# Filling the start of a two-layer decoder trunk: idle transposes, an earlier gate weight, small loads last

## The chip, the cores and the metric

The kernel runs on one core of a Trainium2 chip. What counts is the device time in microseconds (us) of one execution: the median of several.

## The reference

A trunk of two layers on x (1 x 1024 x 1024, float32). Layer 1 mixes tokens with a gated linear recurrence (HGRN2, 8 heads of 128), layer 2 with sliding-window attention; each has a gated feed-forward part behind it, and every sub-layer ends with a layer norm. Only the head of layer 1 matters here:

```python
def hgrn2_mixer(h, w_in, lower_bound, g_norm_w, w_out):
    """h (B,S,D); w_in (D, 4D) = [q | f | i | g] columns"""
    q, f, i, g = jnp.split(h @ w_in, 4, axis=-1)
    ...
    fg = lb + (1.0 - lb) * jax.nn.sigmoid(heads(f))
    o = hgrn2_chunkwise(jax.nn.silu(heads(q)), 1.0 - fg, heads(i), jnp.log(fg))
    o = o * lax.rsqrt(jnp.mean(jnp.square(o), -1, keepdims=True) + RMS_EPS)
    o = o * g_norm_w.astype(jnp.float32) * jax.nn.silu(heads(g))
    return o.reshape(B, S, D).astype(h.dtype) @ w_out
```

So every head needs x times four blocks of 128 columns of `w_in`: i, g, q and f.

## The kernel before, in words

**Tiling.** x is held as eight blocks of 128 rows ("rows 0" to "rows 7"). Every product needs x with the model dimension on the partitions, so each block is transposed on TensorE (`x_block`, through `tr`, L179: eight transposes of 128 x 128 into one PSUM tile `psax`) and then split into a high and a low part in `T` (`split`: ScalarE makes the high part, L196, VectorE the low part, L144). A product of float32 quality is three matmuls, high x high, high x low, low x high (`mm3`, L169 to L171).

**Weights.** A weight block of 512 KB is loaded into one of three `raw` buffers in turn (`load`, L139) and split into one of six slots of `HL` (`split_raw`: ScalarE L151, then VectorE L144; for the first one GpSimd). `ig_load(h, u)` takes half of the model dimension of i and g of head h with two DMAs of 256 KB; `qf_load(h, g)` takes the whole of q (g = 0) or f (g = 1) with one DMA.

**Stages at the beginning.** Rows 0 and 1 are transposed; then the i/g projection of head 0 runs in four blocks of two row blocks each (`ig_block(0, us, tp)`, tp = 0 to 3: "block 0" to "block 3"), with the transposes of the next two row blocks set among its matmuls (`x_pair`, a chain of the `Order` object that steps when the counted TensorE time has passed). A block has 48 matmuls of 256 columns and, for blocks 0 to 2, 16 transposes. Then come the f and q projection of head 0 and, head by head, the recurrence. Between blocks 2 and 3 the parameters (`pr`, 81 x 128) are transposed into `par` (L745), and before that the masks (`mf`) are turned into bytes (`msk`, L743).

**Who sets the order.** Inside `tc.manual_schedule(engines=...)` the named engines keep the order in which the program is written. For engines that aren't named a scheduler chooses the place of each instruction by its own estimate of when it can start; this is so for ScalarE and VectorE where head 0's f and q weights are split, since that code names only TensorE and SyncE. All loads of this stage go through SyncE's queue (SP), in the order written, and eight semaphores take turns: a DMA is only issued when the DMA eight places ahead of it has landed.

The lines around the change in the kernel before:

```python
                ahead = od.spawn(x_pair(2), 2.0)
                ig_block(0, us, 0)
                od.finish([ahead])
                for i, n in enumerate(("hgrn_lb_logits", ...)):
                    nc.sync.dma_start(pr[16 * i:16 * (i + 1), :], ...)
                nc.sync.dma_start(pr[80:81, :], a["hgrn_gnorm_w"])
                for tb in range(4, NB):
                    x_load(tb)
...
            w = {g: qf_split(qf_load(0, k)) for k, g in enumerate("qf")}
```

Of the kernel before, what the change touches and what calls it, by code (L numbers as in the profile page):

```python
# [10 lines left out]
F32 = mybir.dt.float32  # L11
# [5 lines left out]
P = 128  # L17
S = 1024
D = 1024
NB = S // P  # L20
KC = D // P
BL = 32
# [65 lines left out]
def trunk(ctx: ExitStack, tc: tile.TileContext, a: dict, out: bass.AP):  # L88
    nc = tc.nc
# [13 lines left out]
    ident = cp.tile([P, P], F32, name="ident")  # L103
# [11 lines left out]
    def psmm():  # L115
        return mmp.tile([P, 512], F32, name="psmm")

    def psax():
        return axp.tile([P, 1024], F32, name="psax")
# [12 lines left out]
    def hl_at(i):  # L132
        return HL[:, 2 * i:2 * i + 2, :]

    def load(loads):
        raw = tail["raw"][ring["raw"] % 3]
        ring["raw"] += 1
        for view, src in loads(raw):
            nc.sync.dma_start(view, src)  # L139
        return raw  # L140
# [9 lines left out]
    def split_into(hl, raw, eng=None):  # L150
        nc.scalar.copy(hl[:, 0], raw)  # L151
        low_part(hl[:, 1], raw, hl[:, 0], eng)
        return hl

    def split_raw(raw, eng=None):
        ring["hl"] += 1
        return split_into(hl_at((ring["hl"] - 1) % 6), raw, eng)
# [20 lines left out]
    def tr(ps, src):  # L178
        nc.tensor.transpose(ps, src, ident)  # L179
        od.t += 0.109  # L180
# [14 lines left out]
    def split(hi, lo, src, eng=None):  # L195
        nc.scalar.copy(hi, src)  # L196
        return low_part(lo, src, hi, eng)
# [462 lines left out]
    w_in = a["hgrn_w_in"][0]  # L660
    w_iv = w_in.rearrange("(kc p) c -> p kc c", p=P)
    hgrn_pool = tc.tile_pool(name="hp", bufs=1, reuse_waits="tile")
    with tc.tile_pool(name="t", bufs=1, reuse_waits="tile") as raws, hgrn_pool as hp:
        raw_tail(raws)

        def ig_load(h, u):
            return load(lambda r: [(r.rearrange("p (k g c) -> p k g c", k=4, g=2)[:, :, g, :],
                                    w_iv[:, 4 * u:4 * u + 4, (2 + g) * D + h * P:(2 + g) * D + (h + 1) * P])
                                   for g in range(2)])

        def ig_split(raw, eng=None):
            return split_raw(raw, eng).rearrange("p h (k c) -> p h k c", k=4)

        VG = {}

        def ig_block(h, us, tp):
            if tp == 0:
                VG[h] = (hp.tile([P, NB, P], F32, name="V"), hp.tile([P, NB, P], F32, name="G"))
            V, G = VG[h]
            ps = psmm()  # L680
# [16 lines left out]
        with tc.tile_pool(name="ep", bufs=1, reuse_waits="tile") as ep:  # L697
            pr = ep.tile([81, P], F32, name="pr")

            def x_load(tb):  # L700
                nc.sync.dma_start(Y[:, tb, :], x[tb * P:(tb + 1) * P, :])

            def x_block(tb):
                ps = psax()
                for kc in range(KC):
                    tr(ps[:, kc * P:(kc + 1) * P], Y[:, tb, kc * P:(kc + 1) * P])
                ts = slice(tb * P, (tb + 1) * P)
                split(T[:, 0, :, ts], T[:, 1, :, ts], ps.rearrange("p (k t) -> p k t", k=KC))

            def x_pair(tb):  # L710
                yield 0.0
                x_block(tb)
                yield 0.5
                x_block(tb + 1)

            warm = sm.tile([P, 1], F32, name="warm")
            nc.scalar.copy(warm, nhalf)
            with tc.manual_schedule(engines={EN.PE, EN.SP, EN.Activation, EN.DVE}):
                x_load(0)
                raw0 = ig_load(0, 0)  # L720
                x_load(1)
                raw1 = ig_load(0, 1)
                for tb in range(2, 4):
                    x_load(tb)
                us = [ig_split(raw0, nc.gpsimd)]
                x_block(0)
                x_block(1)
                us.append(ig_split(raw1))
                ahead = od.spawn(x_pair(2), 2.0)
                ig_block(0, us, 0)  # L730
                od.finish([ahead])
                for i, n in enumerate(("hgrn_lb_logits", "ln_mix_g", "ln_mix_b", "ln_ffn_g", "ln_ffn_b")):
                    nc.sync.dma_start(pr[16 * i:16 * (i + 1), :], a[n].rearrange("r (k p) -> (r k) p", p=P))
                nc.sync.dma_start(pr[80:81, :], a["hgrn_gnorm_w"])
                for tb in range(4, NB):
                    x_load(tb)
            for tp in range(1, NB // 2 - 1):
                ahead = od.spawn(x_pair(2 * tp + 2), 2.0)
                ig_block(0, us, tp)
                od.finish([ahead])  # L740
            mf = hp.tile([P, 7 * BL + P], F32, name="kd")
            nc.sync.dma_start(mf, a["masks"])
            nc.vector.tensor_copy(msk, mf)  # L743
            ps = psmm()
            nc.tensor.transpose(ps[:, :81], pr, ident[:81, :81])  # L745
            nc.vector.tensor_copy(par, ps[:, :81])
            lm = ep.tile([P, NH], F32, name="lm")
            le = ep.tile([P, 2, NH], F32, name="le")
            nc.vector.tensor_tensor(lm, par[:, 0:8], par[:, 8:16], op=ALU.max)
            for r in range(2):  # L750
                nc.vector.tensor_tensor(le[:, r, :], par[:, 8 * r:8 * r + 8], lm, op=ALU.subtract)
            nc.scalar.activation(le, le, AF.Exp)
            nc.vector.tensor_tensor(lm, le[:, 0, :], le[:, 1, :], op=ALU.add)
            nc.vector.reciprocal(lm, lm)
            nc.vector.tensor_tensor(lbt[:, 0, :], le[:, 0, :], lm, op=ALU.mult)
            nc.vector.tensor_scalar(lbt[:, 1, :], lbt[:, 0, :], -1.0, 1.0, op0=ALU.mult, op1=ALU.add)
            ig_block(0, us, NB // 2 - 1)
# [25 lines left out]
            nc.scalar.dma_start(rbd, rl.unsqueeze(1).to_broadcast([16, P, 2 * P]))  # L783

        params = od.spawn(conv_params())

        def qf_load(h, g):
            wv = w_in.rearrange("(kc p) c -> p kc c", p=P)
            c0 = g * D + h * P
            return load(lambda r: [(r.rearrange("p (k c) -> p k c", k=KC), wv[:, :, c0:c0 + P])])  # L790

        def qf_split(raw):
            return split_raw(raw).rearrange("p h (k c) -> p h k c", k=KC)

        def qf(h, weights):

# [18 lines left out]
        def recur(h, qs, fg, kp):  # L815
# [98 lines left out]
            yield 2.2  # L914
            V, G = VG[h]
            ps = psax()
# [86 lines left out]

        values_done = [-1]
        with tc.manual_schedule(engines={EN.PE, EN.SP}):
            w = {g: qf_split(qf_load(0, k)) for k, g in enumerate("qf")}
            nw, nraw = {}, {g: qf_load(1, k) for k, g in ((1, "f"), (0, "q"))}
            make_w = [lambda g=g: nw.update({g: qf_split(nraw[g])}) for g in "fq"]
            steps = qf(0, w)
            for k in range(4):  # L1010
                slot_begin()
                slot_end(*next(steps), *(make_w[k - 1:k] if k else ()))
            for _ in steps:
                pass
            task = od.spawn(recur(0, *w["out"]))
            w = nw
            for h in range(1, NH):
                us, nw = [], {}
                raws = [ig_load(h, u) for u in range(2)]
                make_ig = [lambda u=u: us.append(ig_split(raws[u])) for u in range(2)]  # L1020
                steps = qf(h, w)
                for make in ((), make_ig[:1], make_ig[1:], ()):
                    slot_begin()
                    slot_end(*next(steps), *make)
                for _ in steps:
                    pass
                if h < NH - 1:
                    nraw = {g: qf_load(h + 1, k) for k, g in ((1, "f"), (0, "q"))}
                    make_w = [lambda g=g: nw.update({g: qf_split(nraw[g])}) for g in "fq"]
                else:  # L1030
                    make_w = []
                for tp in range(NB // 2):
                    if tp == lead[h]:
                        od.finish([task])
                        task = od.spawn(recur(h, *w["out"]))
                    slot_begin()
                    slot_end(*ig_block(h, us, tp), *(make_w[tp - 1:tp] if tp else ()))
                w = nw
# [41 lines left out]
    with (tc.tile_pool(name="ta", bufs=1, reuse_waits="tile") as raws,  # L1080
# [195 lines left out]
        with tc.manual_schedule(engines={EN.PE, EN.Activation, EN.DVE, EN.Pool}):  # L1276
# [12 lines left out]
            g = q_proj(hl)  # L1289
            q, done = next(g)  # L1290
# [11 lines left out]
            for c in range(8):  # L1302
# [31 lines left out]
                q = nq  # L1334
# [58 lines left out]
```

## Time and profile before

| | us |
|---|---|
| median of 3 runs | 2213.2 |
| lowest and highest | 2210.26, 2213.62 |
| the profiled execution | 2211.82 |
| its span | 2209.8 |

The span is the time from the first to the last instruction in the trace; the profiled execution's own time is 2.0 us longer. Times in the views count from the span's start. In a timeline a row is start, duration, engine, line, operation, what is written from what, and in brackets how long the engine was idle before it and what ended that. In a table of windows a row is the stretch, its length, busy time and number of instructions of TensorE's matmuls (PE), weight loads (PEld), VectorE (DVE), ScalarE (ACT) and GpSimd (POOL), then the granted TensorE clock, the DMA engines' share and GB/s. The trace has no record of the clock ahead of 12.17 us, so the column says nothing there.

### The profile page before, as it was taken

The numbers are of one execution on the slowest core, as the hardware profiler recorded it, in microseconds if no ns is written. First come the engines' busy times: TensorE is split into PE (matmuls) and PEld (weight loads), VectorE is DVE, ScalarE is ACT, GpSimd is POOL, SyncE is SP. The second block draws the span as 40 slices with busy tenths as digits, with TensorE's granted clock in tenths as the row PEclk, the third lists the DMA queues.
The fourth block names the chain that finished last, engine by engine and source line by source line (L and its number), as shares of the span: only waits on it lengthen the run. The fifth ranks groups of instructions, "written<-read, shape, count | busy, mean of one in ns | idle before, by whom it ended". The sixth has DMA issues, their size and how long they took to land.

```text
span 2209.8 us, 33157 instructions
## 1 busy us (share of the span) xinstructions
PE 2168.1 (98%) x13007; PEld 1810.5 (82%) x13007; DVE 1777.6 (80%) x2415; ACT 932.1 (42%) x1601; POOL 178.6 (8%) x196
## 2 busy tenths in 40 slices
PE   8999999989999999999999999999999999999998
PEld 7888888878888888887888888878888888887887
DVE  2777665555789888988997779977899888889987
ACT  4333333332744334344343546655654444343431
POOL 0122111110100000000000013211000000000001
PEclk9999999999999999999999999999999999999999
DMA  6565443152223222227954431123123222249663
GB/s 197 173 208 195 161 168 120 48 97 89 96 69 104 86 86 86 86 79 252 303 162 153 106 99 35 34 81 120 67 96 105 80 73 77 86 153 315 202 208 137
DMA packets 231942, 281.14 MB, mean 127 GB/s; under 512 B 29977, under 2 KB 160746, under 8 KB 228970
## 3 DMA queue, kind: packets, MB, share of 16 engines
q1 hardware_dynamic: 228898, 276.57, 38.6%
q10 hardware_dynamic: 2888, 2.45, 0.9%
q8 instruction: 102, 1.67, 0.3%
q14 instruction: 54, 0.44, 0.1%
HBM read 213.96 MB, written 65.01 MB: 126 GB/s over the span
## 4 chain that ended last, share of the span: by engine, by line
PE 82%; DVE 9%; DMA 4%; ACT 3%; issue 2%; POOL 1%; SPq 0%; DVEq 0%; ACTq 0%; POOLq 0%
PE psmm L169 17%; PE psmm L171 17%; PE psmm L170 16%; PE psax L171 8%; PE psax L169 8%; PE psax L170 8%; PE psax L175 3%; DVE T L144 1%; PE psmm L175 1%; PE psax L1185 1%; PE psax L179 1%; DVE HL L144 1%; ACT Y L244 1%; DMA raw<-in_hgrn_w_out_dram 1%; DMA raw<-in_hgrn_w_in_dram 1%
## 5 line engine op out<-in xcount | busy, mean ns | idle before, releaser
L169 PE MATMUL psmm<-T,HL 128*128 128x512 f32 x768 | 307.1, 400 | 0.0
L170 PE MATMUL psmm<-T,HL 128*128 128x512 f32 x768 | 300.2, 391 | 2.1 <-DVE T L144 2.1
L171 PE MATMUL psmm<-T,HL 128*128 128x512 f32 x768 | 300.8, 392 | 0.0
L474 DVE SCALAR_TENSOR_TENSOR Y<-Y,cwt 128x1023 f32<-128x1023 f32 (+1 forms) x176 | 225.3, 1280 | 39.9 <-ACT Y L472 39.7
L472 ACT ACTIVATE Y<-Y,cwt 128x1024 f32<-128x1024 f32 x88 | 109.1, 1240 | 263.6 <-DVE Y L461 260.6
L169 PE MATMUL psmm<-HL,T 128*128 128x256 f32 (+1 forms) x656 | 201.0, 306 | 1.0 <-ACT T L196 1.0
L171 PE MATMUL psmm<-HL,T 128*128 128x256 f32 (+1 forms) x656 | 196.2, 299 | 2.0 <-DVE T L144 2.0
L170 PE MATMUL psmm<-HL,T 128*128 128x256 f32 (+1 forms) x656 | 196.3, 299 | 1.7 <-DVE HL L144 1.7
L196 ACT CAST HL<-rx 128x1024 fp32r<-128x1024 f32 (+1 forms) x137 | 140.3, 1045 | 122.4 <-DMA rx<-in_ffn_w_in_dram 33.3
L144 DVE TENSOR_TENSOR HL<-rx,HL 128x1024 fp32r<-128x1024 f32 (+1 forms) x137 | 165.9, 1213 | 12.3 <-ACT HL L196 12.0
L170 PEld LDWEIGHTS psmm<-T,HL 128*128 128x128 f32 x768 | 144.4, 188 | 31.3 <-DVE T L144 2.9
L169 PEld LDWEIGHTS psmm<-T,HL 128*128 128x128 f32 x768 | 144.3, 188 | 31.1 <-issue 1.2
L171 PEld LDWEIGHTS psmm<-T,HL 128*128 128x128 f32 x768 | 144.1, 188 | 31.0
L171 PE MATMUL psax<-T,HL 128*128 128x512 f32 x352 | 137.6, 391 | 0.0
L169 PE MATMUL psax<-T,HL 128*128 128x512 f32 x352 | 137.5, 391 | 0.0
L170 PE MATMUL psax<-T,HL 128*128 128x512 f32 x352 | 137.4, 390 | 0.0
L169 PEld LDWEIGHTS psmm<-HL,T 128*128 128x128 f32 x656 | 127.4, 194 | 7.8 <-issue 2.9
L171 PEld LDWEIGHTS psmm<-HL,T 128*128 128x128 f32 x656 | 127.2, 194 | 5.9 <-DVE T L144 2.7
L170 PEld LDWEIGHTS psmm<-HL,T 128*128 128x128 f32 x656 | 127.5, 194 | 5.4 <-DVE HL L144 2.1
L218 POOL TENSOR_TENSOR rs<-rs,nhalf 128x1 f32<-128x1 f32 x32 | 26.0, 813 | 1293.2 <-DVE rs L217 1292.9
L850 POOL TENSOR_TENSOR kp<-kp,tot 128x512 f32<-128x512 f32 x48 | 73.6, 1534 | 293.6 <-PE psax L175 151.7
L196 ACT CAST HT<-rx 128x1024 fp32r<-128x1024 f32 (+1 forms) x51 | 44.0, 863 | 89.4 <-PE psmm L170 30.5
(298 smaller groups left out, 5251.5 us busy)
## 6 DMA issues: line engine op xcount, KB each, us to landing
rx<-in_ffn_w_in_dram SPq DMA_DIRECT2D x136, 256.0 KB, 3.4
rx<-gd SPq DMA_DIRECT2D x118, 256.0 KB, 3.5
Y<-in_ffn_w_out_dram SPq DMA_DIRECT2D x44, 512.0 KB, 6.6
bsd<-Y SPq DMA_DIRECT2D x22, 1024.0 KB, 3.9
gd<-Y SPq DMA_DIRECT2D x44, 512.0 KB, 2.7
rx<-in_ffn_w_out_dram SPq DMA_DIRECT2D x54, 256.0 KB, 3.8
R<-bsd SPq DMA_DIRECT2D x44, 256.0 KB, 4.8
Y<-in_ffn_w_in_dram SPq DMA_DIRECT2D x40, 256.0 KB, 3.3
```

The lines of the kernel that those rows point to most:

```text
L144: make = lambda e: e.tensor_tensor(lo, src, hi.bitcast(F32), op=ALU.subtract)
L169: nc.tensor.matmul(ps, st(0), mv(0), start=start, stop=False)
L170: nc.tensor.matmul(ps, st(0), mv(1), start=False, stop=False)
L171: nc.tensor.matmul(ps, st(1), mv(0), start=False, stop=stop)
L175: nc.tensor.matmul(ps, lhsT, rhs, start=start, stop=stop, **kw)
L179: nc.tensor.transpose(ps, src, ident)
L196: nc.scalar.copy(hi, src)
L218: nc.gpsimd.tensor_tensor(rs, rs, nhalf, op=ALU.pow)
L244: nc.scalar.activation(hf[:, kc, :], ps[:, k * P:(k + 1) * P], AF.Identity, bias=shift, scale=scale)
L472: nc.scalar.activation(c, u, AF.Identity, bias=cwt[:, l, 3, ci:ci + 1], scale=cwt[:, l, 2, ci:ci + 1])
L474: nc.vector.scalar_tensor_tensor(c[:, sh:], u[:, :S - sh], cwt[:, l, 2 - sh, ci:ci + 1], c[:, sh:], op0=ALU.mult, op1=ALU.add)
L850: (nc.gpsimd if i else nc.vector).tensor_tensor(kv[:, :, 0, :], kv[:, :, 0, :], tv[:, :, 1:2].to_broadcast([P, nb, m]), op=ALU.mult)
```

## The change

It has three parts, all ahead of the f and q projection of head 0.

1. TensorE gets 33 transposes of the identity matrix into a PSUM tile that no one reads: 13 ahead of the transposes of rows 0, 20 ahead of those of rows 1.
2. Head 0's f weight is loaded behind rows 5 and its q weight behind rows 7, both from within the first stage. Before, q and f were loaded in that order behind the masks. Where they are split isn't written in another place: it is still the dictionary ahead of `steps = qf(0, w)`, now with f first.
3. The six small loads of the parameters, which stood ahead of rows 4, and the load of the masks come behind the q weight. The tile of the masks is reserved earlier.

```diff
+        def qf_load(h, g):
+            c0 = g * D + h * P
+            return load(lambda r: [(r.rearrange("p (k c) -> p k c", k=KC), w_iv[:, :, c0:c0 + P])])
+
+        def qf_split(raw):
+            return split_raw(raw).rearrange("p h (k c) -> p h k c", k=KC)
...
+            mf = hp.tile([P, 7 * BL + P], F32, name="kd")
             with tc.manual_schedule(engines={EN.PE, EN.SP, EN.Activation, EN.DVE}):
...
                 us = [ig_split(raw0, nc.gpsimd)]
-                x_block(0)
-                x_block(1)
+
+                idle = psmm()
+                for tb, n in ((0, 13), (1, 20)):
+                    for _ in range(n):
+                        nc.tensor.transpose(idle[:, :P], ident, ident)
+                    x_block(tb)
                 us.append(ig_split(raw1))
                 ahead = od.spawn(x_pair(2), 2.0)
                 ig_block(0, us, 0)
                 od.finish([ahead])
+                for tb in range(4, 6):
+                    x_load(tb)
+                rawf = qf_load(0, 1)
+                for tb in range(6, NB):
+                    x_load(tb)
+                rawq = qf_load(0, 0)
                 for i, n in enumerate(("hgrn_lb_logits", "ln_mix_g", "ln_mix_b", "ln_ffn_g", "ln_ffn_b")):
                     nc.sync.dma_start(pr[16 * i:16 * (i + 1), :], a[n].rearrange("r (k p) -> (r k) p", p=P))
                 nc.sync.dma_start(pr[80:81, :], a["hgrn_gnorm_w"])
-                for tb in range(4, NB):
-                    x_load(tb)
+                nc.sync.dma_start(mf, a["masks"])
...
-            mf = hp.tile([P, 7 * BL + P], F32, name="kd")
-            nc.sync.dma_start(mf, a["masks"])
             nc.vector.tensor_copy(msk, mf)
...
-            w = {g: qf_split(qf_load(0, k)) for k, g in enumerate("qf")}
+            w = {g: qf_split(raw) for g, raw in (("f", rawf), ("q", rawq))}
```

More of the change, by code (lines that the diff above doesn't have):

```diff
@@ L785, in trunk @@
         params = od.spawn(conv_params())
[L787 to L793, printed above, removed]
         def qf(h, weights):
```

## The prediction

> **What bounds the kernel now.** I read the page first, then the chain of waits in its first 60 us, then each engine's timeline there, then windows of the clock.
>
> ```profile
> span 2209.8 us, 33157 instructions
> PE 2168.1 (98%) x13007; PEld 1810.5 (82%) x13007; DVE 1777.6 (80%) x2415; ACT 932.1 (42%) x1601; POOL 178.6 (8%) x196
> ```
>
> TensorE is busy for 2168.1 of 2209.8 us, so 41.7 us of idleness is all that a change of order can win or add to, apart from the clock. The diff only touches the beginning. Built, the two programs hold the same instructions in the same order on every engine from the gate projection of head 0 on (some waits there name other semaphores). A delay at the beginning is therefore kept to the end, unless something later waits on a fixed time, and nothing there does: the later loads are released by engines that shift along. Here is the beginning in the chain of waits and on TensorE:
>
> ```profile
> 7.24 6.88 DMA Y<-in_x_dram
> ...
> 16.73 9.84 DMA raw<-in_hgrn_w_in_dram
> 26.60 1.06 ACT HL L151
> 27.68 1.23 DVE HL L144
> 28.90 1.15 DVE T L144
> 30.09 0.38 PE psmm L171
> ```
>
> ```profile
> 4.94 1.94 PE L179 MATMUL psax<-ident,Y 128*128 128x128 f32 x8 [4.94 <-DMA Y<-in_x_dram]
> 8.47 1.97 PE L179 MATMUL psax<-ident,Y 128*128 128x128 f32 x8 [1.59 <-DMA Y<-in_x_dram]
> 10.45 0.53 PE L170 MATMUL psmm<-HL,T 128*128 128x256 f32 x1
> 12.59 0.28 PE L169 MATMUL psmm<-HL,T 128*128 128x256 f32 x1
> 13.93 0.38 PE L170 MATMUL psmm<-HL,T 128*128 128x256 f32 x1 [1.06 <-DVE HL L144]
> 15.34 1.03 PE L179 MATMUL psax<-ident,Y 128*128 128x128 f32 x8
> 27.34 0.28 PE L171 MATMUL psmm<-HL,T 128*128 128x256 f32 x1
> 28.61 0.38 PE L169 MATMUL psmm<-HL,T 128*128 128x256 f32 x1 [0.99 <-ACT T L196]
> 30.09 0.38 PE L171 MATMUL psmm<-HL,T 128*128 128x256 f32 x1 [0.98 <-DVE T L144]
> 37.45 0.23 PE L745 MATMUL psmm<-ident,pr 81*128 81x81 f32 x1
> ```
>
> Two things hold TensorE up. Eight transposes take 1.94 us at first and 1.03 us later: until about 12 us it runs at half speed. And at 27.5 us it stands before block 2 of the i/g projection (rows 4 and 5 of x), for 2.6 us. The chain says why: a gate weight load of head 0 lands at 26.57, ScalarE splits it (L151), and the split of x row 4 (L196, then L144 on VectorE) stands behind it in the same queues. From the landing to TensorE's L171 are 30.09 - 26.57 = 3.52 us. Block 2 then takes 37.45 - 30.09 = 7.36 us.
>
> **The change part by part.**
>
> *Idle transposes.* The identity is ready at about 1.4 us:
>
> ```profile
> 1.14 0.29 POOL masks.py:199 TENSOR_SCALAR_AFFINE_SELECT ident<-ident 128x128 f32<-128x128 f32 x1
> ```
>
> 13 transposes at 1.94 / 8 = 0.24 us end at 1.4 + 3.2 = 4.6 us, before x row 0 at 4.94; the 20 others at 1.03 / 8 = 0.13 end near 8.5, when row 1 arrives. If the clock rises late they run at 0.24, and block 1's transposes start up to 1.7 us late (bound). If it rises in time, row 1's transposes end 0.95 us sooner, and this goes through ScalarE:
>
> ```profile
> 10.47 1.01 ACT L196 CAST T<-psax 128x1024 fp32r<-128x1024 f32 x1 [1.66 <-PE psax L179]
> 11.38 1.05 ACT L151 CAST HL<-raw 128x1024 fp32r<-128x1024 f32 x1
> 20.16 0.37 ACT L684 COPY V<-psmm 128x256 f32<-128x256 f32 x1 [1.14 <-PE psmm L171]
> 26.60 1.05 ACT L151 CAST HL<-raw 128x1024 fp32r<-128x1024 f32 x1 [1.72 <-DMA raw<-in_hgrn_w_in_dram]
> 27.55 1.92 ACT L196 CAST T<-psax 128x1024 fp32r<-128x1024 f32 x2
> ```
>
> The cast of row 1 and the split of the second i/g weight run back to back, so TensorE's restart at 13.93 comes at about 13.0, and block 0 ends at about 19.2 instead of 20.15 (when ScalarE's L684 takes its result). Gain so far 0.95 us.
>
> *Weights ahead of the last rows.* This is the part that decides. The scheduler places ScalarE's and VectorE's splits of head 0's f and q weights where it thinks that they fit. Before, they stand behind block 0's output and ahead of the splits of rows 4 and 5. In the changed program both stand further ahead: ScalarE's order is split of the second i/g weight, split of f, split of q, and only then the casts of rows 2 and 3. VectorE's is the same. Block 1 of the projection needs row 2 and now waits for the load of q, as block 2 did before. Yet q is loaded last, behind all eight rows. So the stall of before isn't removed; it moves one block ahead, to a load that hardly comes sooner.
>
> When does q land? Ahead of it and with it are 12 transfers of 512 KB (eight rows, four weights): 6.29 MB, with 0.13 MB of ScalarE's own loads 6.42 MB.
>
> ```profile
> 0.00:12.25 12.25, 5.72 (x26) 5.31 (x27) 1.96 (x2) 5.21 (x6) 4.38 (x11) 1.00 0.86 262
> 12.25:14.75 2.50, 1.44 (x13) 1.24 (x12) 1.62 (x2) 0.18 (x1) 0.00 (x0) 1.00 0.45 120
> 14.75:22.75 8.00, 8.00 (x71) 8.00 (x70) 3.10 (x4) 4.07 (x5) 0.00 (x0) 1.00 0.99 334
> 22.75:26.60 3.85, 3.85 (x36) 3.85 (x35) 1.25 (x2) 1.05 (x2) 0.00 (x0) 1.00 1.00 254
> 30.00:38.00 8.00, 7.91 (x67) 7.91 (x68) 4.15 (x6) 2.41 (x5) 0.00 (x0) 1.00 0.93 369
> ```
>
> ```profile
> 12.89 2.54 SPq L701 DMA_DIRECT2D Y<-in_x_dram  x4
> ```
>
> The last column of the windows is GB/s. By 12.25 us 262 x 12.25 = 3.21 MB are there. Before, the queue then ran nearly dry (120 GB/s), as SP, with six small loads issued ahead, issued row 4 only at 12.89, when row 2 had landed; the change closes this gap by putting the small loads behind. The other 3.21 MB take 9.6 us at 334 GB/s: 21.9 us. At 369 it is 20.95, at 254 24.9. I add 0.9 us for the last of the 16 engines (x row 3 landed at 7.24 + 6.88 = 14.12, when the queue had been slack for almost 2 us, so its last pieces lagged by more than that allowance; if such a lag doesn't recur, nothing): q lands at 22.8, between 21.0 and 25.0. SP's other waits lie before: q overwrites the first i/g weight, whose last reader is done at 10.35:
>
> ```profile
> 7.98 2.37 POOL L144 TENSOR_TENSOR HL<-raw,HL 128x1024 fp32r<-128x1024 f32 x1 [5.40 <-ACT HL L151]
> ```
>
> Block 1's L171 then comes at 22.8 + 3.52 = 26.3 and TensorE stands from 19.2 to 24.8 (the first L169, 1.5 us ahead as at 28.61), does two matmuls and waits again. Block 2 starts 7.36 us later at full speed: 33.7 against 30.09, which is 3.6 us late. The 0.95 us won by the idle transposes is lost in that wait: block 0 merely ends earlier in front of it.
>
> *The clock.* A stand of over 5 us has a price of its own. The trace shows a place in which the granted clock fell (column 1.00 or 0.50; the window's length stands first, then TensorE's busy time):
>
> ```profile
> 474.45 1.08 PE L175 MATMUL psax<-og,one 128*32 128x256 f32 x8 [3.74 <-DVE og L865]
> ```
>
> ```profile
> 469.55:472.97 3.42, 1.15 (x20) 0.58 (x18) 0.20 (x1) 1.84 (x4) 0.00 (x0) 1.00 0.16 60
> 472.97:476.38 3.41, 1.93 (x12) 1.12 (x13) 3.41 (x5) 3.41 (x6) 1.82 (x1) 0.50 0.00 0
> 476.38:479.79 3.41, 3.41 (x18) 3.41 (x18) 3.41 (x5) 0.91 (x3) 0.31 (x1) 0.50 0.00 0
> 25.82:29.23 3.41, 2.30 (x17) 1.89 (x16) 1.87 (x3) 2.63 (x3) 0.00 (x0) 1.00 0.58 158
> ```
>
> The clock goes in stretches of 3.41 us. A stretch with 1.15 us of TensorE work brought half speed in the next one, one with 2.30 us did not; a wholly busy stretch gave it back, one with 1.93 us did not. With TensorE idle from 19.2 to 24.8 and again to 26.3, the last stretch that ends before 26.3 has at most 0.7 us of work wherever its edges lie: block 1 starts at half speed. It stays so until the end of a stretch with enough work. If anything over 1.93 us is enough, that is 1.9 us after 26.3 at the earliest; if it takes a whole stretch, 6.8 us at the latest. Half of this is lost: 1.0 to 3.4, 2.2 in the middle.
>
> The Trainium skill, TensorE: Matmul & The Clock Gate, "Part 1: The HAM clock gate", has the clock fall only after at least one idle window of about 3.4 us, free-running. By that sentence a stand of 5.6 us would hold a whole window in 64% of cases (an estimate from the page's window), and the sum would be 3.6 in the others. The trace's rows speak for a stricter gate: the stand of 3.74 us before 474.45 left 1.15 us of work in the stretch in which it began, and that was enough.
>
> *Small loads and masks behind.*
>
> ```profile
> 22.10 0.34 DVE L743 CAST msk<-kd 128x352 uint8<-128x352 f32 x1 [1.83 <-DMA kd<-in_masks_dram]
> 26.16 0.37 SPq L139 DMA_DIRECT2D raw<-in_hgrn_w_in_dram  x1
> 54.91 1.04 ACT L151 CAST HL<-raw 128x1024 fp32r<-128x1024 f32 x1
> ```
>
> The masks, formerly at 22.1 us on VectorE, follow q by about a microsecond and are used on VectorE behind rows 2 and 3; the parameters are transposed after block 2. Price 0, hidden by blocks 1 and 2; without this cover 1 us. The last load of the next head's weights is issued behind the masks rather than at 26.16, and its first user comes at 54.91. The idle transposes take one more of four psmm buffers in turn, which are all free then: price 0. The down-projection rows behind them wait for transposes of x, so they shift with TensorE.
>
> **Sum.** 22.8 + 3.52 + 7.36 + 2.2 - 30.09 = +5.8 us. The profiled execution took 2211.8 us (span 2209.8), 1.4 below the median of 2213.2; to the median it makes 2219.0. The ends are 21.0 + 3.52 + 7.36 + 1.0 - 30.09 = +2.8 and 25.0 + 3.52 + 7.36 + 3.4 - 30.09 = +9.2.
>
> **The rivals.** (1) *The clock holds*: the stand falls across an edge, so that no stretch is idle enough, and the price is 3.6, 2216.8. For it: a single fall is shown, and its limit lies anywhere between 1.15 us and far less. Against it: in every position the stand leaves a stretch with under 0.7 us. (2) *No stall, the faster side*: q lands so early that block 1 isn't held. Then 0.95 us at the start and 27.46 to 30.09 less two matmuls' 0.24, 2.4 us, before block 2 are won: -3.3, 2209.9. The point of decision is a landing at 19.2 - 3.52 = 15.7 us for the whole of it, and 30.09 - 7.36 - 3.52 = 19.2 for a draw; that asks for 3.21 MB in 7 us, 460 GB/s, where the rows have 369 at most. Small chance, unless ScalarE's queue runs otherwise than the program's order, which no row suggests: at 26.60 and 27.55 it kept it. (3) *A second stand*: the 2.4 us before block 2 stay beside the new ones, since row 4's splits follow those of rows 2 and 3 on both queues, and the half clock takes its longest: 3.6 + 2.4 + 3.4 = +9.4, 2222.6. Against it: those queues have all of block 1, 7.36 us, to catch up. (4) *The idle transposes don't raise the clock*: no difference to the sum, since the wait for q covers it.
>
> **How the numbers follow.** Forecast 0.70, (1) 0.12, (2) 0.10, (3) 0.08. Under 0.2%, 4.4 us, this kernel can't be told from no change (its three runs lie 3.4 us apart). Of the forecast's span of 2.8 to 9.2 about four fifths lie above 4.4: 0.57, with (3) 0.65 slower. Same: the rest of the forecast 0.13, (1) 0.12 and half of (2): 0.30. Faster: half of (2), as the runs scatter, 0.05. The range leaves out (2) and half of (3): 2214.5 to 2222.5, from 2.3 us below rival (1) to the forecast's upper end.
>
> **What would show it.** Right: in the changed timeline ScalarE's second and third L151 of gate weights stand before the cast of row 2, the last one released by a DMA at 22 to 24 us; TensorE idle from about 19 to 25; the clock column 0.50 behind it; eight transposes of row 0 or at latest row 1 in about 1 us; block 2 starting at 35 to 37 us, without the stand at 27.5. Wrong: q at or before 19 us, block 1 that starts at 19, or a stand with the clock still 1.00.

## The result and the profile after

| | before | after |
|---|---|---|
| median | 2213.41 us (14 runs) | 2217.84 us (14 runs) |
| lowest and highest | 2209.92, 2217.89 | 2215.02, 2222.68 |
| profiled execution, its span | 2211.82, 2209.8 | 2220.28, 2218.2 |

The ratio is 1.0021, interval 1.0014 to 1.0028: the changed kernel is slower by 4.4 us. A second comparison (below) gave 1.0017. Both intervals exclude no change, but the size of the first lies on the bound of 0.2% that the prediction drew, and that of the second below it.

The span and the busy time of each engine, from the page of the kernel after:

```profile
span 2218.2 us, 33224 instructions
PE 2173.5 (98%) x13040; PEld 1814.9 (82%) x13040; DVE 1776.9 (80%) x2415; ACT 930.6 (42%) x1601; POOL 179.4 (8%) x196
```

There are 33 more matmul instructions; TensorE's idle time goes from 41.7 us to 2218.2 - 2173.5 = 44.7. The chain of waits in the first 60 us of the kernel after, the pieces ahead of the first matmul of block 1 (start, duration, what):

```profile
9.78 4.12 SPq L708
13.94 0.43 SPq L708
14.49 9.33 DMA raw<-in_hgrn_w_in_dram
23.84 1.05 ACT HL L151
24.92 1.23 DVE HL L144
26.14 1.15 DVE T L144
27.33 0.58 PE psmm L171
```

It is the chain of before with another head: the same four steps from a landed gate weight to L171, now ahead of block 1. The weight is q and lands at 14.49 + 9.33 = 23.82 us. The issue of rows 6 took SP 4.12 us, so q was issued only at 14.49. TensorE's timeline of the kernel after:

```profile
1.49 2.98 PE L738 MATMUL psmm<-ident 128*128 128x128 f32 x13 [1.49 <-POOL ident masks.py:199]
8.35 1.09 PE L179 MATMUL psax<-ident,Y 128*128 128x128 f32 x8 [0.31 <-DMA Y<-in_x_dram]
12.94 0.38 PE L170 MATMUL psmm<-HL,T 128*128 128x256 f32 x1 [0.90 <-DVE HL L144]
25.85 0.58 PE L169 MATMUL psmm<-HL,T 128*128 128x256 f32 x1 [6.72 <-ACT T L196]
27.33 0.58 PE L171 MATMUL psmm<-HL,T 128*128 128x256 f32 x1 [0.69 <-DVE T L144]
36.79 0.28 PE L171 MATMUL psmm<-HL,T 128*128 128x256 f32 x1
```

The idle transposes do raise the clock (row 1's eight take 1.09 us), and the restart comes at 12.94. Then TensorE stands for 6.72 us ahead of block 1, and block 1 takes 36.79 - 27.33 = 9.46 us. ScalarE's timeline shows who holds it:

```profile
10.55 1.05 ACT L151 CAST HL<-raw 128x1024 fp32r<-128x1024 f32 x1
19.17 1.04 ACT L151 CAST HL<-raw 128x1024 fp32r<-128x1024 f32 x1 [7.57 <-DMA raw<-in_hgrn_w_in_dram]
23.84 1.04 ACT L151 CAST HL<-raw 128x1024 fp32r<-128x1024 f32 x1 [3.63 <-DMA raw<-in_hgrn_w_in_dram]
24.79 1.92 ACT L196 CAST T<-psax 128x1024 fp32r<-128x1024 f32 x2
```

The splits of f and q (19.17 and 23.84) both stand ahead of the casts of rows 2 and 3 (24.79, two in one row), which need no weight at all. The clock column of the windows of the kernel after:

```profile
17.93:21.34 3.41, 1.20 (x11) 1.00 (x9) 1.10 (x1) 1.04 (x1) 0.00 (x0) 1.00 1.00 330
21.34:24.75 3.41, 0.00 (x0) 0.00 (x0) 0.13 (x1) 0.91 (x1) 0.00 (x0) 0.50 0.33 90
24.75:28.17 3.42, 1.63 (x6) 1.34 (x7) 3.25 (x3) 3.42 (x5) 0.00 (x0) 0.50 0.85 237
28.17:31.58 3.41, 3.41 (x18) 3.41 (x18) 0.91 (x3) 0.49 (x2) 0.00 (x0) 0.50 1.09 377
31.58:34.99 3.41, 3.41 (x31) 3.41 (x31) 0.93 (x1) 1.41 (x2) 0.00 (x0) 1.00 1.00 374
```

Half speed from 21.34 to 31.58 us, so 31.58 - 27.33 = 4.25 us of block 1 run at 0.50. TensorE's busy time grows by 5.4 us over the kernel before.

### The profile page after: what moved, and what is told of

It reads as the page before. It is cut to its first block, busy times and chain, and to the rows that moved or that the text cites. A ratio compares the mean times of both kernels' runs of the same rounds, so it can differ in the third digit from the quotient of the medians.

```text
span 2218.2 us, 33224 instructions
## 1 busy us (share of the span) xinstructions
PE 2173.5 (98%) x13040; PEld 1814.9 (82%) x13040; DVE 1776.9 (80%) x2415; ACT 930.6 (42%) x1601; POOL 179.4 (8%) x196
## 4 chain that ended last, share of the span: by engine, by line
PE 78%; DVE 11%; DMA 4%; ACT 3%; issue 2%; POOL 1%; SPq 0%; DVEq 0%; ACTq 0%; POOLq 0%
PE psmm L169 16%; PE psmm L171 16%; PE psmm L170 16%; PE psax L171 8%; PE psax L169 8%; PE psax L170 8%; PE psax L175 3%; DVE T L144 2%; DVE HL L144 1%; PE psmm L175 1%; PE psax L179 1%; PE psax L1192 1%; ACT Y L244 1%; DVE Y L642 1%; DMA raw<-in_hgrn_w_out_dram 1%
## 5 line engine op out<-in xcount | busy, mean ns | idle before, releaser
L171 PE MATMUL psmm<-T,HL 128*128 128x512 f32 x768 | 300.8, 392 | 0.0
L171 PE MATMUL psmm<-HL,T 128*128 128x256 f32 (+1 forms) x656 | 196.7, 300 | 1.7 <-DVE T L144 1.7
L171 PEld LDWEIGHTS psmm<-T,HL 128*128 128x128 f32 x768 | 144.1, 188 | 31.3 <-issue 0.3
L171 PE MATMUL psax<-T,HL 128*128 128x512 f32 x352 | 137.6, 391 | 0.0
L171 PEld LDWEIGHTS psmm<-HL,T 128*128 128x128 f32 x656 | 127.5, 194 | 5.6 <-DVE T L144 2.5
L144 DVE TENSOR_TENSOR HL<-raw,HL 128x1024 fp32r<-128x1024 f32 x51 | 64.5, 1264 | 23.4 <-ACT HL L151 23.2
```

What stands on the lines that cost most here:

```text
L144: make = lambda e: e.tensor_tensor(lo, src, hi.bitcast(F32), op=ALU.subtract)
L171: nc.tensor.matmul(ps, st(1), mv(0), start=False, stop=stop)
```

## The experiments

The theory: a gate weight's split stands ahead of x rows in the in-order queues of ScalarE and VectorE, so the block of those rows waits for the landing of the weight; the time follows where the splits stand and when the weight lands, and a clock fall comes on top. The rivals: it is the loads' order or their sharing of the DMA engines; it is a chance of the trace; the idle transposes cost as such; the parts add up independently. "Start" is the first L171 of block 2, the 30.09 us of before: all that the change does lies ahead of it or hides in it. Ratios are to the kernel before in runs on the same chip.

**The pair again.** No edits.

> The kernel before once more, for a second profile. Both theories: block 2 of the i/g projection starts (its first L171) at 30.1 us give or take 0.7, as the f weight lands near 26.6. What is open is the later part: how long TensorE stands near 470 and 483 us and where the granted clock falls there; if these differ by a microsecond or two from the first profile, single profiles can't be compared beyond the beginning.

> The changed kernel once more. Queue theory (the splits of f and q stand ahead of rows 2 and 3 on ScalarE and VectorE): block 1's first L171 comes 3.5 us behind the landing of q, the clock is 0.50 for 3.4 to 10 us from about 21 to 22 us on, block 2 starts at 35.5 to 38 us (36.8 in the first profile). Rival (the loss arises later, around 470 to 580 us, where the first pair of profiles drifts by another 2 us): block 2 start varies little but the later drift comes back at the same place and size.

Measured: before again 0.9997 (0.9985 to 1.0008), start 31.34; after again 2218.88 against 2215.32 us, 1.0017 (1.0007 to 1.0028). TensorE's timelines of before again (first fence) and of after again:

```profile
31.34 0.39 PE L171 MATMUL psmm<-HL,T 128*128 128x256 f32 x1 [0.98 <-DVE T L144]
```

```profile
13.72 0.39 PE L170 MATMUL psmm<-HL,T 128*128 128x256 f32 x1 [1.06 <-DVE HL L144]
25.53 0.58 PE L169 MATMUL psmm<-HL,T 128*128 128x256 f32 x1 [5.63 <-ACT T L196]
36.51 0.28 PE L171 MATMUL psmm<-HL,T 128*128 128x256 f32 x1
```

The stand and the late start come again; the restart of block 0 does not (13.72, against 12.94 in the first profile). The start of one and the same kernel moves by over a microsecond from one profile to the next (30.09, 31.34, the second outside what I expected), which bounds what the start of a single profile can tell. The change's start is late by 6.70 us in the first pair of profiles and 5.17 in the second, 5.9 in the mean. The rival that the loss arises later is refuted: the stand of TensorE that ends at 474.45 us in the first profile of before ends at 475.99 in the second, and at 482.35 and 481.44 in the kernel after, 7.9 and 5.5 us later in the two pairs. Most of that is there at block 2, and none of it has been given back by then.

**The splits held back.** Loads, idle transposes and TensorE's order of the kernel after; only the two splits are tied behind block 2's output.

```diff
-                ig_block(0, us, tp)
+                held = ig_block(0, us, tp)
...
-            w = {g: qf_split(raw) for g, raw in (("f", rawf), ("q", rawq))}
+            with tc.issue_after(held[0].ins), tc.issue_after(held[1].ins):
+                w = {g: qf_split(raw) for g, raw in (("f", rawf), ("q", rawq))}
```

> The changed kernel with one edit: the splits of head 0's f and q weights are tied behind block 2's output, so that ScalarE and VectorE split rows 2 to 5 first; loads and TensorE's order are those of the changed kernel. Queue theory: no stand at 19 us, block 1 starts at 19.1, block 2 at 26.5, block 2 ends at 33.9 (37.45 before, 44.05 after the change); the time is 3.5 us under the kernel before, near 2210, and 8 to 10 under the changed one. Rival (it is the load order: weights ahead of the last rows hold up the rows, or the idle transposes cost TensorE time): the start stays at 35 us or more, and the time at 2217.

> The changed kernel with the splits tied behind block 2's output, once more, beside the two kernels with small products. Queue theory: block 2 starts at 26.5 to 27.5 us, and the time is 5 to 8 us under the kernel before, near 2208. Rival (the first runs of it were lucky): 2210 or more.

Measured: 0.9961 (0.9947 to 0.9974) and again, on another chip, 0.9975 (0.9964 to 0.9986). ScalarE's timeline of the first of the two, and TensorE's of the second:

```profile
17.73 1.01 ACT L196 CAST T<-psax 128x1024 fp32r<-128x1024 f32 x1 [0.57 <-PE psax L179]
32.72 1.01 ACT L196 CAST T<-psax 128x1024 fp32r<-128x1024 f32 x1 [0.57 <-PE psax L179]
35.41 1.05 ACT L151 CAST HL<-raw 128x1024 fp32r<-128x1024 f32 x1
37.90 1.03 ACT L151 CAST HL<-raw 128x1024 fp32r<-128x1024 f32 x1
```

```profile
12.96 0.39 PE L170 MATMUL psmm<-HL,T 128*128 128x256 f32 x1 [0.84 <-DVE HL L144]
26.86 0.39 PE L171 MATMUL psmm<-HL,T 128*128 128x256 f32 x1
```

The casts of the rows follow their transposes (17.73, and the last at 32.72), the splits come at 35.41 and 37.90, and neither stand is there: block 2 starts at 26.86 (27.41 in the first). With the same loads the time falls from 2218.88 to 2208.09 us in the same comparison. Where the splits stand is thus worth 10.8 us (9 to 10 by the second run, if the kernel after is taken 3.6 to 4.4 us above the kernel before), more than the whole of the change; the order of the loads by itself can't be the cause. This version beats both kernels. It is 7.2 and 5.4 us under the kernel before, where I had expected 3.5 for the first run. The start is 3.3 and 3.8 us sooner; the rest is taken up below.

**The clock alone.** The kernel after with 60 more idle transposes behind block 0, while TensorE stands anyway.

```diff
                 od.finish([ahead])
+                for _ in range(60):
+                    nc.tensor.transpose(idle[:, :P], ident, ident)
```

> The changed kernel with 60 more transposes of the identity behind block 0, about 6.5 us of work that no one reads, set in the stand of 19.1 to 25.9 us; nothing else differs. Clock theory: the granted clock stays 1.00, block 1 takes 7.4 rather than 9.5 us, block 2 starts at 34.7 rather than 36.8, and the time falls by 2.1 us to about 2215.7. Rival (the half speed in block 1 has another cause, as operands that arrive late): block 1 still takes 9.5 us, and the time is the same or a little worse.

Measured: 2216.91 us, 1.0003 (0.9994 to 1.0012). TensorE's timeline:

```profile
19.22 6.71 PE L745 MATMUL psmm<-ident 128*128 128x128 f32 x60
27.15 0.38 PE L171 MATMUL psmm<-HL,T 128*128 128x256 f32 x1 [0.98 <-DVE T L144]
34.74 0.28 PE L171 MATMUL psmm<-HL,T 128*128 128x256 f32 x1
```

Block 1 starts at 27.15 as without them, but takes 34.74 - 27.15 = 7.59 us instead of 9.46. In the windows its clock column stays at 1.00 there. The time is 2218.88 - 2216.91 = 2.0 us less than that of the kernel after in the same comparison; the intervals of the two ratios just overlap (up to 1.0012, from 1.0007), but the size is the one that block 1 shows. So the stand has the two prices that the prediction gave it, the wait and the clock, and the second is 1.9 to 2.1 us.

**The parts one by one.** Before with the splits tied as above; after with the splits tied and without idle transposes; after without idle transposes; before with the 33 idle transposes.

```diff
-                for tb, n in ((0, 13), (1, 20)):
-                    for _ in range(n):
-                        nc.tensor.transpose(idle[:, :P], ident, ident)
-                    x_block(tb)
+                x_block(0)
+                x_block(1)
```

> The kernel before with the splits of head 0's f and q weights tied behind block 2's output; none of the change's three parts. Queue theory: the stand of 27.5 to 30.1 us goes, block 2 starts at 27.5, and the time is 2.4 us under the kernel before: 2211. Rival (load order): the rows arrive as before, nothing changes, 2213.4.

> The kernel with the splits tied behind block 2's output and the change's loads, without the idle transposes. Queue theory: TensorE runs at half speed till about 12 us again, block 2 starts 0.95 us later than with them, at 27.5; the time is 1 us above that kernel and equal to the kernel before with tied splits, since the order of the loads hides nothing that is waited for. Rival (the order of the loads is worth something by itself): it is over 1 us faster than the kernel before with tied splits.

> The changed kernel without its idle transposes. The scheduler now places f's split ahead of rows 2 and 3, but q's behind them, ahead of rows 4 and 5. Queue theory: block 1 waits for f (landing at 19.1) rather than q: its first L171 at 22.6, the clock keeps 1.00 since the stand is only 2.5 us long, block 2 starts at 30.0 as before the change, and the time is that of the kernel before, 2213.4, give or take 1. Rival (the parts add up, the idle transposes alone give 0.95 us): it is 1 us slower than the changed kernel, 2218.8.

> The kernel before with the 33 idle transposes alone. The scheduler places both splits ahead of block 0's output on ScalarE, so that behind f's landing (26.6) come the split, the output of block 0, a table load and the gate, and only then row 4. Queue theory: block 2 starts at 26.57 + 3.52 + 2.1 = 32.2, and TensorE stands 5 us, which halves the clock for a while: 2 us to 4 us slower than the kernel before, 2215.5 to 2217.5. Rival (the idle transposes do what they say): 1 us faster or no change, as block 0 ends 0.95 us sooner.

| kernel | ratio | interval | start |
|---|---|---|---|
| before, splits tied | 0.9981 | 0.9972 to 0.9990 | 27.82 |
| after, splits tied, no idle transposes | 0.9983 | 0.9973 to 0.9992 | 27.76 |
| after, no idle transposes | 0.9995 | 0.9986 to 1.0004 | 29.41 |
| before, with idle transposes | 1.0005 | 0.9997 to 1.0014 | 34.45 |

The first two differ by the order of the loads alone (with the small loads and the masks), and agree: once no split stands in the way, these runs show no gain from the order of the loads (2210.85 and 2210.35 us). Both came lower than I expected, 2211 against a kernel before of 2213.4: they are 4.6 and 5.1 us under the kernel before, not 2.4. The third leaves out the part that seemed harmless, and the stand ahead of block 1 is gone. Its timelines of ScalarE, and of TensorE:

```profile
18.10 1.05 ACT L151 CAST HL<-raw 128x1024 fp32r<-128x1024 f32 x1 [5.88 <-DMA raw<-in_hgrn_w_in_dram]
19.05 1.92 ACT L196 CAST T<-psax 128x1024 fp32r<-128x1024 f32 x2
23.83 1.04 ACT L151 CAST HL<-raw 128x1024 fp32r<-128x1024 f32 x1
```

```profile
16.22 1.86 PE L179 MATMUL psax<-ident,Y 128*128 128x128 f32 x8
```

Only f's split (18.10) is left ahead of rows 2 and 3; q's stands behind block 0's output. The 33 transposes therefore cost little themselves, but with them the scheduler puts q's split two rows further ahead. The time came as expected (2214.25 us, the same as the kernel before), and refutes that the parts add up (2218.8); the path was another. I had expected a stand of 2.5 us for f. There was none, since f landed a microsecond sooner (18.1) and TensorE came later: row 2's eight transposes at 16.22 still ran at half speed (1.86 us), so that block 0's result was taken at 21.87 rather than 20.16. That the start is near the 30.0 that I expected is luck. The fourth shows the scheduler's choice from the other side: in the kernel before the transposes bring both splits ahead of block 0's output. I expected a start of 32.2 and a time 2 to 4 us above the kernel before; the start came at 34.45, the time can't be told from the kernel before (0.5 us above it), and the mechanism was another: row 4 did not wait for f. The timelines of VectorE, and of TensorE, in that kernel:

```profile
11.88 1.23 DVE L144 TENSOR_TENSOR HL<-raw,HL 128x1024 fp32r<-128x1024 f32 x1 [0.18 <-ACT HL L151]
23.73 0.34 DVE L747 CAST msk<-kd 128x352 uint8<-128x352 f32 x1 [10.62 <-DMA kd<-in_masks_dram]
23.98 2.35 DVE L144 TENSOR_TENSOR T<-psax,T 128x1024 fp32r<-128x1024 f32 x2
```

```profile
25.26 0.58 PE L171 MATMUL psmm<-HL,T 128*128 128x256 f32 x1 [5.66 <-DVE T L144]
```

Here it is the masks' cast to bytes (23.73) that holds rows 2 and 3 on VectorE for 10.62 us. It is the same fault in a third guise: an instruction that waits for a load, ahead of rows that are ready.

**An earlier load.** The kernel after with f and q loaded right behind rows 3.

```diff
-                for tb in range(4, 6):
-                    x_load(tb)
                 rawf = qf_load(0, 1)
-                for tb in range(6, NB):
-                    x_load(tb)
                 rawq = qf_load(0, 0)
+                for tb in range(4, NB):
+                    x_load(tb)
```

> The changed kernel with f and q loaded right behind rows 3, ahead of rows 4 to 7. The scheduler then places both splits ahead of the cast of row 1 and the split of the second i/g weight on ScalarE. Queue theory: q lands near 18 us, block 0 stands after its first 13 matmuls until about 4.8 us behind that (22.5 to 23 rather than 12.9), the clock halves, and block 2 starts near 38.4 rather than 36.5: about 2 us slower than the changed kernel, 2220 to 2221. Rival (an earlier load of q shortens the wait): q lands 5 us sooner, so block 2 starts 5 us sooner, at 31.5, and the time is 2213.5.

Measured: 2221.22 us, 1.0030 (1.0019 to 1.0042), the slowest of all, with the start at 38.78, close to what I expected. ScalarE's and TensorE's timelines:

```profile
16.72 1.04 ACT L151 CAST HL<-raw 128x1024 fp32r<-128x1024 f32 x1 [7.96 <-DMA raw<-in_hgrn_w_in_dram]
18.48 1.04 ACT L151 CAST HL<-raw 128x1024 fp32r<-128x1024 f32 x1 [0.72 <-DMA raw<-in_hgrn_w_in_dram]
19.44 1.00 ACT L196 CAST T<-psax 128x1024 fp32r<-128x1024 f32 x1
```

```profile
21.44 0.58 PE L169 MATMUL psmm<-HL,T 128*128 128x256 f32 x1 [9.52 <-ACT HL L151]
23.11 0.58 PE L170 MATMUL psmm<-HL,T 128*128 128x256 f32 x1 [1.08 <-DVE HL L144]
38.78 0.28 PE L171 MATMUL psmm<-HL,T 128*128 128x256 f32 x1
```

q lands 5.3 us sooner (18.48), and the splits move ahead as well, now in front of row 1's cast (19.44) and the second i/g weight: block 0 stands for 9.52 us. The rival that an earlier weight helps is refuted for this program, because the place of the split moves with the load.

**Other idle work.** The versions with tied splits gain more with the 33 transposes (0.9961, 0.9975) than without (0.9983). To tell the clock from the mere count of instructions I used small products, 32 x 32, instead: 33 ahead of rows 0, or 108 in place of the 13.

```diff
+                for _ in range(33):
+                    nc.tensor.matmul(idle[:32, :32], ident[:, :32], ident[:, :32], start=True, stop=True)
```

> The kernel with tied splits and the change's loads, without the idle transposes, but with 33 products of 32 x 32 instead, ahead of row 0: as many instructions in TensorE's stream as the idle transposes, next to no time, and no warming of the clock up to row 1. Fetch theory (TensorE's instructions are loaded in pieces of 16 KB by the DMA engines that also load the weights; 66 more instructions move these loads against the program, away from a load that TensorE waits for near 1041 and 2009 us): block 2 starts at 27.8 as without any idle work, but the instruction load moves from 4.4 to some 10 us ahead of the stand near 1041 us, the stand falls from 1.9 to 0.9 us, and the time is 2 us under the same kernel without the 33, near 2208.5. Rival (the later part differs by chance, by where the clock's windows fall): no difference, 2210.4.

> The kernel with tied splits, the change's loads and the 20 idle transposes ahead of row 1, but 108 products of 32 x 32 in place of the 13 ahead of row 0: 128 more matmuls in all, 256 instructions with their weight loads, which is one whole piece of 16 KB. Fetch theory: the instruction loads come back to where they were without any idle work, 4.4 us ahead of the stand near 1041 us, the stand is 1.5 to 2.5 us again, and the time is about 2 us above that with 33 transposes, 2210; block 2 starts at 27.4, or up to 2 us later if the 108 products take longer than the 3.3 us until row 0 is there. Rival (the idle work helps later by something that any number of it gives, as a buffer more in the turn of PSUM): as with 33 transposes, 2208.1.

Measured: 0.9984 (0.9975 to 0.9993), start 27.31, and 0.9996 (0.9987 to 1.0005), start 33.08. The first time, 2210.41 us, is that of the rival (chance, by where the clock's windows fall) and not that of the fetch theory; neither run decides it. TensorE's timelines of the two:

```profile
1.48 3.73 PE L736 MATMUL psmm<-ident 128*32 128x32 f32 x66 [1.48 <-POOL ident masks.py:199]
```

```profile
1.48 8.28 PE L736 MATMUL psmm<-ident 128*32 128x32 f32 x216 [1.48 <-POOL ident masks.py:199]
```

Each of these float32 products became two matmuls, so both counts were twice what I meant (66 and 216), and the 108 took 8.28 us, past the arrival of rows 0, which delayed the whole start. Nor does the first tell the clock from the count: the 66 raised the clock as well (row 1's eight transposes take 1.09 us there, not 1.97), which I had not expected. What it shows: the gain that I expected from the count of instructions is not in its times.

## Why the prediction was right, and where it was not

The forecast was 2219.0 us, with "slower" as likeliest; the median is 2217.84. Step by step:

- **Idle transposes, 0.95 us sooner, covered by the wait.** Right in the first profile: restart 12.94 us against 13.0 forecast. In the second it is 13.72: row 0's eight transposes still take 1.97 us there. The two profiles with tied splits show the same two cases once nothing covers the gain (restarts 13.66 and 12.96, starts 27.41 and 26.86, against 27.8 without the transposes). Full clock begins at 4.27 us in the first profile of the kernel after and at 7.46 in the second, so 0.95 was the better of two cases. Without idle work it begins at 11.7 to 12.2 us in three profiles and only at 17.5 and 17.9 in two (before again; after without the transposes), and the transposes take away this late rise as well. What this step missed: I put the new place of the splits down to the loads' order, and the runs without and with the transposes alone show that q's place depends on the transposes.
- **The splits ahead of rows 2 and 3, on both queues.** Right, and shown by the two versions that hold them back: it is the cause of the stand.
- **q lands at 22.8 us.** It was 23.82 (23.5 in the second profile). The view of the DMA engines in the first 25 us of the kernel after, in 40 slices of 0.625 us:

```profile
GB/s 0 0 26 47 284 406 339 343 329 354 363 286 312 291 252 261 265 295 321 302 374 393 419 392 370 352 351 357 391 403 400 321 315 217 112 64 50 218 74 4
```

  The first 35 slices add up to 10,243 x 0.625 us = 6.40 MB by 21.9 us, of the 6.42 that I counted (6.46 with the six small loads). So the transfer's term of 21.9 was right, and the mis-sized one is the lag of the last pieces: 1.9 us instead of 0.9, in which the DMA engines move 64 and 50 GB/s. "SP's other waits lie before" was wrong, too: the issue of rows 6 held SP for 4.12 us and q went out at 14.49. The bulk was on time all the same, since the queue stayed full meanwhile. Whether that late issue makes the lag longer wasn't tried.
- **From the landing to L171, 3.52 us.** Measured 27.33 - 23.82 = 3.51.
- **The clock, 2.2 us, between 1.0 and 3.4.** Measured 9.46 - 7.36 = 2.1, and 2.0 by the times with the stand filled.
- **Sum at block 2, +5.8.** Measured 5.9 in the mean of two pairs of profiles (6.70 and 5.17); that the mean comes so close is luck, as the pairs differ by 1.5.
- **"A delay at the beginning is therefore kept to the end."** This step failed. In the two comparisons the end came 4.4 and 3.6 us late, not 5.9: some 2 us are given back behind block 2. Its condition, that nothing later waits on a fixed time, leaves out the clock, whose stretches of 3.41 us do not shift along with the program (full clock begins at 4.27 us in one profile of the kernel after and at 7.46 in the other).

Against a mean start of before of 30.7 us, the start and the time went like this (start: of one profile; time: difference of medians in the same comparison, so that a row is good to a microsecond or two):

| kernel | start | time | time less start |
|---|---|---|---|
| after; after again | +6.1; +5.8 | +4.4; +3.6 | -1.7; -2.2 |
| after, stand filled | +4.0 | +1.6 | -2.4 |
| before with idle transposes | +3.7 | +0.5 | -3.2 |
| early loads | +8.1 | +7.2 | -0.9 |
| splits tied; again | -3.3; -3.8 | -7.2; -5.4 | -3.9; -1.6 |
| before, splits tied | -2.9 | -4.6 | -1.7 |
| splits tied, no idle transposes | -2.9 | -5.1 | -2.2 |
| after, no idle transposes | -1.3 | -1.2 | +0.1 |
| splits tied, 33 small products | -3.4 | -3.6 | -0.2 |
| splits tied, 108 small products | +2.4 | -0.4 | -2.8 |

With the 33 transposes (the table's first rows, down to "splits tied; again") the last column is -0.9 to -3.9, -2.3 in the mean; in the three without any idle work it is +0.1 to -2.2. It isn't a delay that is caught up, as it has the same sign in kernels that start sooner. What it goes with, in every profile, is the clock behind block 2. There it falls to 0.50 for two, three or four stretches of 3.41 us in all, around 472 to 500 us and in some kernels also at 1042 to 1048 or at 2011 us:

| half speed behind block 2 | profiles | span less start |
|---|---|---|
| 6.8 us | splits tied, both; before with idle transposes; both with small products | 2178.0 to 2179.8 |
| 10.2 us | before; after, both; stand filled; early loads; before, splits tied | 2179.5 to 2181.5 |
| 13.7 us | before again; splits tied, no idle transposes; after, no idle transposes | 2181.9 to 2184.2 |

The means of the groups are 2178.8, 2180.7 and 2183.1, so a stretch goes with some 2 us. The seven profiles with the 33 transposes have 2.6 such stretches in the mean, the five without any idle work 3.6: one stretch, the size of what is missing. (The three rows without any idle work, -1.3 in the mean with as many stretches as the kernel before, fit this less well.) Two windows of the version with tied splits and no idle transposes show such a fall:

```profile
1039.18:1042.59 3.41, 0.74 (x3) 0.30 (x3) 1.77 (x3) 1.04 (x1) 0.00 (x0) 1.00 0.82 297
1042.59:1046.00 3.41, 3.41 (x9) 2.65 (x10) 3.41 (x4) 2.10 (x2) 0.00 (x0) 0.50 0.74 223
```

Why the clock falls less often with the transposes isn't shown. One place that differs lies near 1040 us, where ScalarE's split of a feed-forward weight waits for its load. ScalarE's timelines of the kernel before, and of the version with tied splits:

```profile
1040.95 1.05 ACT L196 CAST T<-rd 128x1024 fp32r<-128x1024 f32 x1 [6.16 <-DMA rd<-in_ffn_w_out_dram]
```

```profile
1037.93 1.05 ACT L196 CAST T<-rd 128x1024 fp32r<-128x1024 f32 x1 [4.54 <-DMA rd<-in_ffn_w_out_dram]
```

The DMA view of the kernel before, from 1035 to 1039.5 us, has this among its queues (packets, MB, share of the engines' time):

```profile
q8 instruction: 1, 0.02, 1.3%
```

One transfer of kind "instruction" falls into the wait for this weight, also in the version with tied splits and no idle transposes; in that with tied splits and idle transposes there is none from 1033 to 1037.5. It is so in all fourteen profiles: in the five without any idle work the wait is 6.1 to 7.3 us and such a transfer falls into it, in the nine others it is 4.0 to 5.6 us and none does. A longer program could thus move the loading of its code away from this weight. But the kernel with 33 small products, which is longer as well, doesn't show the gain in its times, though it has the short wait and the two stretches in its profile, which is of the fastest of its eleven runs; and no run moved the transfer alone. In the profiles what is given back goes with the clock; what makes it fall less often stays open.

Of the rivals, "the clock holds" is refuted (0.50 in both profiles), and so are "no stall" and that the transposes don't raise the clock; the second stand ahead of block 2 did not come. That the total comes out 1.2 us beside the forecast is partly luck: q's landing was put 1 us too early, and the end of the kernel 2 us too late.

## What to carry to other kernels

Where a scheduler places what you don't name, the cost of an edit is in the order that comes out: look in each in-order queue for an instruction that waits for a load, and for ready work behind it. Here tying two splits behind the blocks that don't need them was worth some 10 us, while moving their loads was worth nothing, or cost more. A stand of TensorE can have a second price, the clock (here 2 us), which idle work in the stand takes away. And an edit at the beginning can change how often the clock falls later: before a difference of 2 us is explained by the place of the edit, count the stretches at half speed behind it.

## What the runs showed of the hardware

**The clock falls without a whole idle stretch.** In the kernel after the stretch from 17.93 to 21.34 us holds 1.20 us of TensorE work, and the next is at 0.50. Over all fourteen traces, each of the 50 falls follows a stretch with at most 1.73 us of TensorE work (108 small products, 14.82 to 18.23), and the least work in a stretch without a fall behind it is 1.60 us (splits tied again, from 2195.97). To get the full clock back took more: stretches with up to 2.92 us of work left it at half (before with idle transposes, 479.49 to 482.90), and those with 2.97 or more gave it back (splits tied, no idle transposes, 482.80 to 486.21). The Trainium skill, TensorE: Matmul & The Clock Gate, "Part 1: The HAM clock gate", asks for a whole idle window; the trace disagrees, as in the case with 1.15 us in the prediction.

**The issue of a load can hold its queue.** In the kernel after SP spent 4.12 us on the issue of the row block of 512 KB that begins at 9.78 us, and 0.43 on the next, at 13.94.

**A small float32 product isn't one matmul.** Each 32 x 32 product appears as two, and 108 of them took 8.28 us, 77 ns each.
